# Wider value stripes: 512 columns of weights from rings of five places in the projection phase of a hybrid streaming encoder

## The chip, the cores and the metric

The kernel runs on one core of a Trainium2 chip. The metric is device time in microseconds (us) of one execution, taken as the median of several. Five engines work side by side, each with its own in-order queue: PE (TensorE, matmuls, with PEld its weight loads), DVE (VectorE), ACT (ScalarE), POOL (GpSimd) and SP (SyncE, which here issues nearly all DMAs).

## The reference

One layer of an encoder is computed for a prompt of 16 meta and 2048 prompt tokens and for 8 sample streams of 16 tokens. What matters here:

```
h = layer_norm(x, ln_in_g, ln_in_b)
(g_q, g_k, g_v, g_low, g_r, d_q, d_k, d_v, i_q, i_k, i_w, d_z, m_a, m_b) = split(h @ w_in)
o_a = gla_recurrence(g_q * DK ** -0.5, g_k, g_v, log_sigmoid(g_low @ gla_w2 + gla_gate_b) / 16)
y_a = (rms_norm(o_a) * gla_norm_g * silu(g_r)) @ w_gla
score = sum_h i_w[h] * relu(i_q[h] . layer_norm(i_k)); keep the top 256 keys of each query
y_b = (softmax_attention(d_q, d_k, d_v, kept keys) * silu(d_z)) @ w_dsa
y = layer_norm(ALPHA * h + (sigmoid(m_a + b0) * y_a + sigmoid(m_b + b1) * y_b) @ w_out)
```

The input projection `h @ w_in` has 1024 rows of contraction and 8280 columns. Its parts g_v (values), g_r (value gates) and d_z (z) have 1024 columns each.

## The kernel before

The kernel is written with a tile framework: tiles come from pools with a stated number of buffers, and a scheduler sets the order on each engine from program order, priorities (`early`, `later`) and its own estimate of when operands and places are free. All matrix products have float32 accuracy by splitting each operand into a high and a low part and adding three products (`mm3`, lines 261 to 267: high times high is L265, then the two mixed products; their sum over 8 slices of 128 rows is 24 matmuls).

Phase 1 (`phase1`, `project`) makes the input projection. The 17 blocks of 128 tokens and the 16 meta tokens lie in six pieces of three blocks or so (`PIECES`). `phase_keys` normalises and transposes every piece and makes the keys. Then three groups of two pieces each (`GROUPS`) go through all other columns. A piece's transposed tokens, high and low, stand in one of three pools xp0 to xp2 (`xtiles`, slots fixed by a list; a whole piece, all 8 slices, in one place). Two kinds of stripe exist:

- transposed stripes (`stripe_t`, `tsp`): the weights are the stationary operand, the tokens (256 or 384) stream past; used for gq, gk, q, ma, mb and the index queries;
- natural stripes (`natural`, `nat`): a block of 128 tokens is the stationary operand, 256 columns of weights stream past; used for gv, gr and z, four stripes each in every group, 6 or so blocks per stripe.

`weights` (L240) loads a stripe of w_in in four DMAs of 128x512 into `raw` (three places), casts it to `whi` on ACT (L159) and subtracts on POOL to get `wlo` (L144). Two places exist for whole stripes. Results leave PSUM through ACT (L156, L159) or DVE; for gr, POOL multiplies by gla_norm_g (L618, `silu_norm`); SP stores them.

Beside the stripes run the index scores (`index_block`, L445: matmul on PE into four PSUM places, relu on ACT, weighting on DVE) and the selection of 256 keys (`select`, a bisection by counts on DVE). They go by sets of blocks: a third or half of the group's stripes stand between one set's scores and the next (`per`).

Phase 2 (`phase2`) attends for blocks 15 to 8 (logits L1129/L1130 on PE, masks and maxima on DVE, exp on ACT, transposes L1065, values L1089). With it goes `side_work`, paced by the count of keys done: `gla_gates` (L682 matmuls with gla_w2, exp and log on ACT, scans on DVE), `attend_sample` (L1182 to L1224), the sample recurrence and 16 prompt chunks. The first 13 of its items are written with `early(EARLY)`:

```
            with self.early(EARLY):
                self.load_keys(upper, 1)
                for _ in range(NEARLY):
                    next(side)
                    items -= 1
            self.load_keys(lower, 0)
```

After block 8 the pools of the side work close, `gla_project` (tiles pd) makes y_a beside the attention of blocks 7 to 0, and `finish` does the rest (pd and fo: merges, output projection, layer norm).

Of the kernel before, what the change touches and what calls it, by code (L numbers as in the profile page):

```python
# [21 lines left out]
P = 128  # L22
# [31 lines left out]
VLATE = 60  # L54
PIECE = 720
# [64 lines left out]
class Trunk:  # L120
    def __init__(self, tc, i, o):
        self.tc, self.nc, self.i, self.o = tc, tc.nc, i, o
        self.turn = 0
        self.spare = self.flip = False
# [106 lines left out]
    def raw(self, n):  # L231
        t = self.ws.tile([P, 2 * PMAX], F32, name="raw", bufs=3)
        return t[:, : 2 * n].rearrange("p (k c) -> p k c", k=2)
# [6 lines left out]
    def weights(self, parts, pool=None, name="", eng=None):  # L240

        nc = self.nc
        width = sum(n for _, n in parts)
        w = self.i["w_in"][0].rearrange("(k p) c -> p k c", p=P)
        if pool is None:
            hi = self.ws.tile([P, KT, width], F32R, name="whi")
            lo = self.ws.tile([P, KT, width], F32R, name="wlo")
        else:
            hi = pool.tile([P, KT, width], F32R, name="whi" + name, tag="sc")
            lo = pool.tile([P, KT, width], F32R, name="wlo" + name, tag="sc")  # L250
        for q in range(4):
            s = slice(2 * q, 2 * q + 2)
            raw = self.raw(width)
            a = 0
            for c, n in parts:
                nc.sync.dma_start(raw[:, :, a : a + n], w[:, s, c : c + n])
                a += n
            self.split_sb(hi[:, s, :], lo[:, s, :], raw, eng)
        return hi, lo
# [14 lines left out]
    def prep_x(self, t, xh, xl, c, keep):  # L274
# [9 lines left out]
        for q in range(2):  # L284
# [5 lines left out]
            self.split(xh[:, s, c : c + r], xl[:, s, c : c + r], ps[:, :, :r])  # L290
# [5 lines left out]
    def nat(self, x, c, r, w):  # L296

        ps = self.pp.tile([P, 512], F32, name="pp")
        (hi, lo), (xh, xl) = w, x
        n = hi.shape[-1]  # L300
        self.mm3(ps[:r, :n], lambda k: xh[:, k, c : c + r], lambda k: xl[:, k, c : c + r],
                 lambda k: hi[:, k, :], lambda k: lo[:, k, :], KT)
        return ps[:r, :n]

    def tsp(self, x, c, n, w, a):

        ps = self.pp.tile([P, 512], F32, name="pp")
        (hi, lo), (xh, xl) = w, x
        self.mm3(ps[:, :n], lambda k: hi[:, k, a : a + P], lambda k: lo[:, k, a : a + P],
                 lambda k: xh[:, k, c : c + n], lambda k: xl[:, k, c : c + n], KT)  # L310
# [1179 lines left out]
```

## Time and profile before

| what | before |
|---|---|
| median of 3 runs | 3590.39 us (3590.21 to 3593.11) |
| profiled execution | 3593.96 us, span 3592.2 us |
| PE busy / weight loads busy | 97% / 89% of the span |
| DVE, ACT, POOL busy | 70%, 40%, 30% |
| granted PE clock, mean | 0.991 |
| DMA | 457.77 MB, mean 127 GB/s |

The page gives busy time as the union of instruction durations. On PE a matmul's duration overlaps the next one's, so the distance between two starts tells what one costs. The rows that the prediction uses stand in their own section below.

### The profile page before, as it was taken

The numbers are of one execution on the slowest core, as the hardware profiler recorded it, in microseconds if no ns is written. First come the engines' busy times: TensorE is split into PE (matmuls) and PEld (weight loads), VectorE is DVE, ScalarE is ACT, GpSimd is POOL, SyncE is SP. The second block draws the span as 40 slices with busy tenths as digits, with TensorE's granted clock in tenths as the row PEclk, the third lists the DMA queues.
The fourth block names the chain that finished last, engine by engine and source line by source line (L and its number), as shares of the span: only waits on it lengthen the run. The fifth ranks groups of instructions, "written<-read, shape, count | busy, mean of one in ns | idle before, by whom it ended". The sixth has DMA issues, their size and how long they took to land. (4 is left out here: it accounts for less than half of the span.)

```text
span 3592.2 us, 66024 instructions
## 1 busy us (share of the span) xinstructions
PE 3483.6 (97%) x24196; PEld 3212.5 (89%) x24196; DVE 2528.4 (70%) x5813; ACT 1450.9 (40%) x3092; POOL 1088.8 (30%) x1412
## 2 busy tenths in 40 slices
PE   7999999999999998999999999999999999989999
PEld 6999999999999998998887788888877888879998
DVE  7737998799999998964436677676765666544444
ACT  4435223433324323322535556566565344331110
POOL 3122242242342334434411345455410000022221
PEclk9999999999999999999999999999999999999999
DMA  8642443254442345445573433333343345564431
GB/s 265 202 131 82 139 121 108 83 157 127 119 145 73 103 134 148 140 134 159 171 199 94 122 109 97 102 105 99 100 121 88 89 120 135 151 192 136 124 115 62
DMA packets 550340, 457.77 MB, mean 127 GB/s; under 512 B 95248, under 2 KB 522528, under 8 KB 550016
## 3 DMA queue, kind: packets, MB, share of 16 engines
q1 hardware_dynamic: 550016, 453.56, 43.9%
q8 instruction: 190, 3.11, 0.4%
q14 instruction: 134, 1.10, 0.1%
HBM read 292.49 MB, written 160.92 MB: 126 GB/s over the span
## 5 line engine op out<-in xcount | busy, mean ns | idle before, releaser
L144 POOL TENSOR_TENSOR wlo<-raw,whi 128x512 fp32r<-128x512 f32 x360 | 482.3, 1360 | 817.1 <-ACT whi L159 706.7
L150 DVE TENSOR_SCALAR_CACHE_REDUCE junk<-sc,cand 128x272 bf16<-128x272 f32 (+6 forms) x512 | 701.6, 1370 | 16.9
L265 PE MATMUL pp<-whi,xh 128*128 128x256 f32 (+3 forms) x1952 | 562.1, 288 | 3.5 <-ACT whi L159 2.3
L265 PE MATMUL pp<-xh,whi 128*128 128x384 f32 (+2 forms) x1728 | 563.6, 326 | 1.9 <-ACT whi L159 1.1
L267 PE MATMUL pp<-whi,xl 128*128 128x256 f32 (+3 forms) x1952 | 560.8, 288 | 4.4 <-DVE xl L144 4.4
L267 PE MATMUL pp<-xh,wlo 128*128 128x384 f32 (+2 forms) x1728 | 563.0, 327 | 1.0 <-POOL wlo L144 1.0
L266 PE MATMUL pp<-xl,whi 128*128 128x384 f32 (+2 forms) x1728 | 563.4, 326 | 0.0
L266 PE MATMUL pp<-wlo,xh 128*128 128x256 f32 (+3 forms) x1952 | 561.9, 288 | 0.0
L265 PEld LDWEIGHTS pp<-whi,xh 128*128 128x128 f32 (+1 forms) x1952 | 371.9, 191 | 12.7 <-issue 4.3
L267 PEld LDWEIGHTS pp<-whi,xl 128*128 128x128 f32 (+1 forms) x1952 | 371.0, 190 | 11.3 <-DVE xl L144 6.9
L266 PEld LDWEIGHTS pp<-wlo,xh 128*128 128x128 f32 (+1 forms) x1952 | 371.5, 190 | 7.8 <-issue 5.2
L1131 DVE CUSTOM_DVE_ANT_0 lgl<-pl,mkl 128x348 f32<-128x348 f32 (+8 forms) x608 | 296.1, 510 | 102.8 <-PE pl L1130 65.8
L265 PE MATMUL pd<-xh,wh 128*128 128x242 f32 (+3 forms) x1152 | 327.7, 285 | 8.2 <-ACT wh L1347 4.5
L159 ACT CAST whi<-raw 128x512 fp32r<-128x512 f32 (+1 forms) x344 | 199.2, 622 | 319.7 <-DMA raw<-in_w_in 204.8
L265 PEld LDWEIGHTS pp<-xh,whi 128*128 128x128 f32 x1728 | 325.1, 188 | 3.3 <-ACT whi L159 1.7
L267 PEld LDWEIGHTS pp<-xh,wlo 128*128 128x128 f32 x1728 | 324.8, 188 | 2.5 <-POOL wlo L144 1.8
L266 PE MATMUL pd<-xl,wh 128*128 128x242 f32 (+3 forms) x1152 | 324.6, 282 | 2.1 <-DVE xl L144 2.1
L266 PEld LDWEIGHTS pp<-xl,whi 128*128 128x128 f32 x1728 | 325.1, 188 | 0.6
L267 PE MATMUL pd<-xh,wl 128*128 128x242 f32 (+3 forms) x1152 | 324.5, 282 | 0.8 <-POOL wl L144 0.8
L156 ACT ACTIVATE lgl<-lgl,mx 128x1040 f32<-128x1040 f32 (+7 forms) x256 | 249.9, 976 | 177.9 <-DVE mx L1133 171.4
L1129 PE MATMUL pl<-kd,q 128*128 128x348 f32 (+14 forms) x800 | 302.5, 381 | 14.1 <-DVE mx L1131 4.9
L1130 PE MATMUL pl<-kd,q 128*128 128x348 f32 (+14 forms) x800 | 261.7, 330 | 0.0
(252 smaller groups left out, 7592.7 us busy)
## 6 DMA issues: line engine op xcount, KB each, us to landing
raw<-in_w_in SPq DMA_DIRECT2D x360, 256.0 KB, 3.2
q<-d_q SPq DMA_DIRECT2D x272, 128.0 KB, 3.0
d_h<-x SPq DMA_DIRECT2D x17, 512.0 KB, 3.3
d_gv<-en SPq DMA_DIRECT2D x68, 128.0 KB, 1.9
d_gr<-en SPq DMA_DIRECT2D x68, 128.0 KB, 2.0
d_z<-en SPq DMA_DIRECT2D x68, 128.0 KB, 1.7
v<-d_gv SPq DMA_DIRECT2D x17, 512.0 KB, 3.7
gr<-d_gr SPq DMA_DIRECT2D x17, 512.0 KB, 3.6
```

The costliest lines, as they stand in the source:

```text
L144: (eng or self.nc.vector).tensor_tensor(out, a, b, op=op)
L150: (eng or self.nc.vector).tensor_scalar(out, a, s1, s2, op0=op0, op1=op1, **kw)
L156: self.nc.scalar.activation(out, a, f, **kw)
L159: (self.nc.vector.tensor_copy if self.spare else self.nc.scalar.copy)(out, src)
L265: mm(ps, ah(k), bh(k), start=k == 0, stop=False)
L266: mm(ps, ah(k), bl(k), start=False, stop=False)
L267: mm(ps, al(k), bh(k), start=False, stop=k == n - 1)
L1129: nc.tensor.matmul(ps[:, :m], q[:, u, :], kd, start=True, stop=False)
L1130: nc.tensor.matmul(ps[:, :m], q[:, 2 + u, :], kd, start=False, stop=True)
L1131: nc.vector.tensor_tensor_reduce(lg[z1][:, a : a + m], ps[:, :m], mk[z1][:, a : a + m], 1.0, NEG, OP.add, OP.max, mx[:, s : s + 1])
```

## The change

- gv, gr and z go in stripes of 512 columns (two per group instead of four); a block's matmul streams 512 columns and fills a PSUM bank; its eviction, its multiply on POOL and its store have 512 columns.
- Weight places hold 1024 columns' worth per partition, five high and five low (`RING`): four slices of a 256-column stripe or two slices of a 512-column stripe. A 256-column stripe takes two places, a 512-column stripe four. `raw` has four places instead of three.
- A piece's tokens lie as two halves of four slices, in one ring of five places (high and low) instead of three whole-piece pools; the fixed slots and the reversed last stripe of the second group (`flip`) go.
- The number of steps per group falls from 28 to 22, so `per` falls from 14 to 11 in the first two groups.

```diff
-        t = self.ws.tile([P, 2 * PMAX], F32, name="raw", bufs=3)
+        t = self.ws.tile([P, 2 * PMAX], F32, name="raw", bufs=RAWB)
...
-        if pool is None:
-            hi = self.ws.tile([P, KT, width], F32R, name="whi")
-            lo = self.ws.tile([P, KT, width], F32R, name="wlo")
...
+        each = 1024 // width if pool is None else KT
+        hi, lo = [], []
+        for q in range(0, KT, each):
+            for x, name in (hi, "whi"), (lo, "wlo"):
+                if pool is None:
+                    t = self.ws.tile([P, 1024], F32R, name=name, bufs=RING)
+                    x.append(t[:].rearrange("p (k c) -> p k c", c=width))
...
+            two = 2 if 2 * width <= 2 * PMAX else 1
+            for k in range(0, each, two):
+                raw = self.raw(width)[:, :two]
+                a = 0
+                for c, n in parts:
+                    nc.sync.dma_start(raw[:, :, a : a + n], w[:, q + k : q + k + two, c : c + n])
+                    a += n
+                self.split_sb(hi[-1][:, k : k + two, :], lo[-1][:, k : k + two, :], raw, eng)
...
     def xtiles(self):
-        q = self.slots.pop(0)
-        return [self.xp[q].tile([P, KT, PMAX], F32R, name="x" + n) for n in "hl"]
+
+        return list(zip(*([self.xp.tile([P, 4, PMAX], F32R, name="x" + n) for n in "hl"] for _ in range(2))))
...
-        for q in GROUPS[g][:: -1 if self.flip else 1]:
+        for q in GROUPS[g]:
...
-            self.xp = [c.enter_context(tc.tile_pool(name=f"xp{q}", bufs=1)) for q in range(3)]
+            self.xp = c.enter_context(tc.tile_pool(name="xp", bufs=5))
...
-            w = self.weights([(col, 256)])
+            w = self.weights([(col, 512)])
...
-                evac(e[:r, :256], ps)
-                nc.sync.dma_start(self.d[dst][COL[t] : COL[t] + r, col - base : col - base + 256], e[:r, :256])
+                evac(e[:r], ps)
+                nc.sync.dma_start(self.d[dst][COL[t] : COL[t] + r, col - base : col - base + 512], e[:r])
...
-            "gv": (4, lambda c: natural(C_GV + c, "gv", C_GV, True, self.copy)),
+            "gv": (2, lambda c: natural(C_GV + c, "gv", C_GV, True, self.copy)),
...
+        wide = "gv", "gr", "z"
+        steps = [lambda n=n, c=(512 if n in wide else 256) * q: step(n, c) for n in order for q in range(kinds[n][0])]
```

The scheduler makes other orders of it. Three places follow; line numbers of the change are 7 or so higher (L267, L682 and L1129 of before are L275, L689 and L1136 of the change, and the load of L976 is at L983).

First, PE where the gate matmuls (pg<-gl,w) start, before: in the last group, among the 256-column blocks of gv.

```order
L265 MATMUL pp<-whi,xh 128x256
L266 MATMUL pp<-wlo,xh 128x256
L267 MATMUL pp<-whi,xl 128x256
L682 MATMUL pg<-gl,w_20247 128x400 x2
L265 MATMUL pp<-whi,xh 16x256
```

The same place of PE in the change: the last transposed stripe of phase 1 ends, and the logits of block 15 follow.

```order
L273 MATMUL pp<-xh,whi 128x384
L274 MATMUL pp<-xl,whi 128x384
L275 MATMUL pp<-xh,wlo 128x384
L689 MATMUL pg<-gl,w_17493 128x400 x4
L1136 MATMUL pl<-kd_18595,q 128x348
L1137 MATMUL pl<-kd_18595,q 128x348
```

Before, 152 rows of the side work stand on PE ahead of the last projection matmul; in the change none does.

Second, SP around the load of gla_w2 (w), which the gate matmuls read, before: among the stores of the merge gates, with many projection loads behind it.

```order
L429 DMA d_mb<-ea 128x256 [waits DMAHW5_49,Activation_49]
L256 DMA raw<-in_w_in 128x2x256 [waits DMAHW6_49,Pool_49]
L172 DMA q<-d_q 64x4x128 [waits DMAHW7_49]
L172 DMA q<-d_q 64x4x128 [waits DMAHW0_49]
L976 DMA w_20247<-in_gla_w 16x512 [waits DMAHW1_49]
L978 DMA gb<-in_gla_gate_b 128x4x1 [waits DMAHW2_49]
L429 DMA d_mb<-ea 128x384 [waits DMAHW3_49,Activation_49]
```

And in the change: behind the last-but-one store of the query heads, right ahead of the load of the lower keys (kd), and waiting for PE.

```order
L174 DMA d_q<-eh 128x384 [waits DMAHW3_49,Activation_49]
L174 DMA d_q<-el 128x384 [waits DMAHW4_49,DVE_49]
L983 DMA w_17493<-in_gla_w 16x512 [waits DMAHW5_49,PE_49]
L985 DMA gb<-in_gla_gate_b 128x4x1 [waits DMAHW6_49]
L174 DMA d_q<-eh 128x384 [waits DMAHW7_49,Activation_49]
L174 DMA d_q<-el 128x384 [waits DMAHW0_49,DVE_49]
L989 DMA lmf<-in_c_levels 128x864 [waits DMAHW1_49]
L174 DMA kd_18595<-d_kd 128x2x1040 [waits DMAHW2_49]
```

The load has moved from the middle of the last group to the end of phase 1.

Third, PE where one gr stripe ends and the next begins (the first group of the change; pp_4967 is the last block of the old stripe, pp_5036 and pp_5065 the first two blocks of the new one, whi_4996 and whi_5006 its first two places).

```order
L275 MATMUL pp_4967<-whi_4812,xl_1921 128x512
L273 MATMUL pp_5036<-whi_4996,xh_1566 128x512
L274 MATMUL pp_5036<-wlo_4997,xh_1566 128x512
L275 MATMUL pp_5036<-whi_4996,xl_1567 128x512
L273 MATMUL pp_5036<-whi_4996,xh_1566 128x512
L274 MATMUL pp_5036<-wlo_4997,xh_1566 128x512
L275 MATMUL pp_5036<-whi_4996,xl_1567 128x512
L273 MATMUL pp_5036<-whi_5006,xh_1566 128x512
L273 MATMUL pp_5065<-whi_4996,xh_1566 128x512
L274 MATMUL pp_5065<-wlo_4997,xh_1566 128x512
L275 MATMUL pp_5065<-whi_4996,xl_1567 128x512
L274 MATMUL pp_5036<-wlo_5007,xh_1566 128x512
```

Before, the blocks of a stripe follow one another whole; in the change the first two blocks of this stripe alternate by place.

## Rows read from the trace of the kernel before

**Rows 1.** The page: span, and busy time, share and instructions of each engine.

```profile
span 3592.2 us, 66024 instructions
...
PE 3483.6 (97%) x24196; PEld 3212.5 (89%) x24196; DVE 2528.4 (70%) x5813; ACT 1450.9 (40%) x3092; POOL 1088.8 (30%) x1412
```

**Rows 2.** Stretches: from:to, length; busy by engine (x instructions); PE clock; DMA.

```profile
130.00:1370.00 1240.00, 1229.89 (x8236) 1219.46 (x8235) 1070.06 (x1632) 450.38 (x953) 399.21 (x333) 1.00 0.41 120
1450.00:1673.00 223.00, 221.36 (x1639) 220.40 (x1638) 154.26 (x387) 50.07 (x100) 84.53 (x66) 1.00 0.50 146
1673.00:1859.00 186.00, 182.91 (x1209) 163.54 (x1208) 79.71 (x154) 94.97 (x150) 65.09 (x42) 0.97 0.59 170
1877.00:2628.00 751.00, 734.66 (x5064) 608.52 (x5064) 520.10 (x1833) 444.26 (x952) 329.68 (x639) 1.00 0.37 103
2628.00:2746.00 118.00, 109.06 (x814) 88.07 (x813) 70.00 (x266) 70.76 (x155) 12.81 (x29) 0.99 0.40 108
2746.00:3164.00 418.00, 409.95 (x3319) 364.13 (x3318) 255.34 (x845) 174.21 (x386) 31.50 (x130) 1.00 0.46 122
3164.00:3592.00 428.00, 408.17 (x2629) 371.81 (x2627) 198.57 (x357) 70.65 (x147) 90.54 (x99) 0.98 0.41 127
```

**Rows 3.** One line's matmuls: count, ns min/median/max, first and last start us, forms.

```profile
L1129 PE MATMUL pl<-kd,q x800: 220/390/800, 1866.9 to 3164.0; 128*128 128x348 f32 x96, 128*128 128x344 f32 x16, 128*128 128x456 f32 x7, 128*128 128x328 f32 x7
...
L902 PE MATMUL pg<-v,kn x128: 377/379/484, 2070.8 to 2629.4; 128*128 128x256 f32 x128
```

**Rows 4.** Timeline, PE, a value stripe of 256 columns: start, duration, instruction.

```profile
500.29 0.28 PE L265 MATMUL pp<-whi,xh 128*128 128x256 f32 x1
...
501.37 0.28 PE L265 MATMUL pp<-whi,xh 128*128 128x256 f32 x1
```

**Rows 5.** Timeline, PE, last stage, 512 columns.

```profile
3559.66 0.39 PE L265 MATMUL fo<-woh,mgh 128*128 128x512 f32 x1
...
3561.93 0.39 PE L266 MATMUL fo<-wol,mgh 128*128 128x512 f32 x1
```

**Rows 6.** PE by line and shape, whole run: xcount, busy us, mean ns, idle.

```profile
L265 PE MATMUL pp<-whi,xh 128*128 128x256 f32 x1632 | 464.9, 285 | 0.3 <-DVE el L144 0.3
```

**Rows 7.** PE groups by line and shape, 1673 to 1859 us.

```profile
L265 PE MATMUL pp<-whi,xh 128*128 128x256 f32 x121 | 36.0, 298 | 0.0
L265 PE MATMUL pp<-xh,whi 128*128 128x384 f32 x96 | 33.0, 344 | 0.0
...
L265 PE MATMUL pp<-xh,whi 128*128 128x256 f32 x96 | 27.1, 283 | 0.0
L682 PE MATMUL pg<-gl,w 16*128 16x512 f32 x24 | 13.4, 640 | 0.9 <-DVE gx L150 0.9
L265 PE MATMUL pp<-whi,xh 128*16 128x256 f32 x24 | 6.7, 277 | 0.0
```

**Rows 8.** Timeline, PE, a transposed stripe, 384 columns.

```profile
401.81 0.33 PE L267 MATMUL pp<-xh,wlo 128*128 128x384 f32 x1
...
402.68 0.33 PE L266 MATMUL pp<-xl,whi 128*128 128x384 f32 x1
```

**Rows 9.** POOL by line and shape, 0 to 1700 us.

```profile
L144 POOL TENSOR_TENSOR wlo<-raw,whi 128x512 fp32r<-128x512 f32 x332 | 442.9, 1354 | 755.6 <-ACT whi L159 665.2 <-DVE whi L159 20.2 <-PE pi L446 18.9
L144 POOL TENSOR_TENSOR en<-en,gng 128x256 f32<-128x256 f32 x68 | 54.5, 802 | 113.0 <-ACT en L156 108.3 <-DMA cd<-in_cache_idx_k 3.4 <-DMA raw<-in_w_in 1.3
```

**Rows 10.** DMA issues: queue, count, KB each, median us to landing.

```profile
raw<-in_w_in SPq DMA_DIRECT2D x360, 256.0 KB, 3.2
```

**Rows 11.** Waits of PE, 0 to 1900 us: total, times, longest.

```profile
PE pi L445 <- ACT rl L156: 18.8, 14, 4.2
```

**Rows 12.** Timeline, PE, end of the projections: [idle before <-releaser].

```profile
1858.72 0.34 PE L267 MATMUL pp<-xh,wlo 128*128 128x384 f32 x1
...
1866.89 0.66 PE L1129 MATMUL pl<-kd,q 128*128 128x348 f32 x1 [2.62 <-DMA kd<-d_kd]
```

**Rows 13.** ACT by line and shape, 1673 to 1859 us.

```profile
L156 ACT ACT_TABLE_LOAD x21 | 26.9, 1283 | 0.4
```

More of the change, by code (lines that the diff above doesn't have):

```diff
@@ L54 @@
 VLATE = 60
+RING = 5
+RAWB = 4
 PIECE = 720
@@ L123, in __init__ @@
         self.turn = 0
-        self.spare = self.flip = False
+        self.spare = False
     @contextmanager
@@ L231, in raw @@
     def raw(self, n):
-        t = self.ws.tile([P, 2 * PMAX], F32, name="raw", bufs=3)
-        return t[:, : 2 * n].rearrange("p (k c) -> p k c", k=2)
+        t = self.ws.tile([P, 2 * PMAX], F32, name="raw", bufs=RAWB)
+        two = 2 if n <= PMAX else 1
+        return t[:, : two * n].rearrange("p (k c) -> p k c", k=two)
     def split_sb(self, hi, lo, src, eng=None):
@@ L244, in weights @@
         w = self.i["w_in"][0].rearrange("(k p) c -> p k c", p=P)
-        if pool is None:
-            hi = self.ws.tile([P, KT, width], F32R, name="whi")
-            lo = self.ws.tile([P, KT, width], F32R, name="wlo")
[L248 to L259, printed above, removed]
+        each = 1024 // width if pool is None else KT
[5 more added lines that the diff above has]
+                    x.append(t[:].rearrange("p (k c) -> p k c", c=width))
+                else:
+                    x.append(pool.tile([P, KT, width], F32R, name=name + str(width), tag="sc"))
+            two = 2 if 2 * width <= 2 * PMAX else 1
[6 more added lines that the diff above has]
+                self.split_sb(hi[-1][:, k : k + two, :], lo[-1][:, k : k + two, :], raw, eng)
+        return (lambda k: hi[k // each][:, k % each, :]), (lambda k: lo[k // each][:, k % each, :]), width
     def mm3(self, ps, ah, al, bh, bl, n):
@@ L289, in prep_x @@
             s = slice(4 * q, 4 * q + 4)
-            self.split(xh[:, s, c : c + r], xl[:, s, c : c + r], ps[:, :, :r])
+            self.split(xh[q][:, :, c : c + r], xl[q][:, :, c : c + r], ps[:, :, :r])
             if keep is not None:
@@ L579, in phase1 @@
             self.inb = self.bcast_load(kp, i["idx_kn_b"][0], 64, "inb")
-            self.x, self.slots = {}, [0, 1, 2, 0, 1, 2, 0, 1, 2, 1]
+            self.x = {}
             self.phase_keys()
@@ L596, in project @@
                     nc.sync.dma_start(raw, self.d["xt"][q][:, k : k + 2, :])
-                    self.split_sb(xh[:, k : k + 2, :n], xl[:, k : k + 2, :n], raw)
+                    r = slice(k % 4, k % 4 + 2)
+                    self.split_sb(xh[k // 4][:, r, :n], xl[k // 4][:, r, :n], raw)
         tiles = [(t, q) for q in GROUPS[g] for t in PIECES[q]]
@@ L634, in step @@
             self.spare = g == len(GROUPS) - 1 and n in SPARE
-            self.flip = g == len(GROUPS) - 2 and (n, c) == (order[-1], 256 * (kinds[n][0] - 1))
             kinds[n][1](c)
-            self.spare = self.flip = False
-        steps = [lambda n=n, c=256 * q: step(n, c) for n in order for q in range(kinds[n][0])]
+            self.spare = False
+        wide = "gv", "gr", "z"
+        steps = [lambda n=n, c=(512 if n in wide else 256) * q: step(n, c) for n in order for q in range(kinds[n][0])]
         blocks = [t for t, _ in tiles if t not in ("m", "s", 0)]
```

19 lines of the change are left out of this document (9 added, 10 removed).

## The prediction

> **What bounds the kernel now.** I read the page first, then busy time by stretch, then the start times on PE, then the waits. The page shows PE busy 97% of the span and its weight loads 89% [rows 1], but the share is not the same everywhere. Cut into stretches [rows 2], the projection phase from 130 to 1370 us and from 1450 to 1673 us has matmuls busy 99% and weight loads 98% to 99% at a granted clock of 1.00 (the 2.4 GHz level): there PE is the bound, and a matmul saved is time saved. Phase 2's attention runs from the first logits at 1866.9 us to the last at 3164.0, and the side work's last prompt chunk ends near 2629 [rows 3]. From 1877 to 2628 us, attention with side work, matmuls still read 98% (734.7 of 751) but weight loads only 81% (608.5 of 751); from 2746 to 3164 us weight loads are at 87%.
>
> What a matmul costs is the distance between two starts. In a value stripe of 256 columns nine distances take 501.37 - 500.29 = 1.08 us, 0.120 us each [rows 4]. In the last stage, with 512 columns and the same 128x128 stationary operand, ten take 2.27 us, 0.227 us each [rows 5]. So two of 256 cost 0.240 us and one of 512 costs 0.227: 0.013 us is a fixed part that a matmul pays whatever its width.
>
> **Term 1, the wider stripes: -32 us.** Three products of 1632 matmuls of 256 columns stand in the trace [rows 6], 4896 in all. The change makes 2448 of 512 columns: 2448 x 0.013 = 31.8 us less. The work lies where PE is the bound. Bounds: none of it if the fixed part comes back as a wait, 32 if all stays.
>
> The page "TensorE: Matmul & The Clock Gate" of the Trainium skill, section Back-to-back issue gap, gives a fixed part of 2.5 ns per matmul when the array is warm; by that the term would be 2448 x 2.5 ns = 6 us instead of 32. The starts in the trace measure 13 ns here, and they decide.
>
> **Term 2, the end of phase 1 loses its guests: -49 us.** This is not in the diff but in the order of the instructions. Before, the load of gla_w2 stands among the last group's projections, and gate and sample-attention matmuls run between projection matmuls; in the change the load waits for PE at the end of phase 1 and no row of the side work stands ahead of the last projection matmul. What the guests take now: in the 186 us from 1673 to 1859 us [rows 2] PE has three products of about 121 natural matmuls, 96 transposed ones of 384 columns, 96 of 256 and 24 for the meta rows [rows 7]. At 0.120 us for 256 columns and 0.87/5 = 0.174 us for 384 [rows 8] that is 363 x 0.120 + 288 x 0.174 + 288 x 0.120 + 72 x 0.120 = 137 us. The other 49 us are guests and the waits around them, and leave phase 1.
>
> **Term 3, the guests' new place: +35 us.** The same work comes back beside the attention of blocks 15 to 8, pushes the remaining side work later, and so pushes the first pass of gla_project, whose pools open when the side work's close, into the stretch after it. Lower bound 0: weight loads leave 19% of 751 us free there, 142 us. Upper bound on PE 49, on ACT more (rival B). I take 35, nearer the upper end, for two reasons: gla_project's displaced pass lands between 2746 and 3164 us, where weight loads are at 87%, and matmuls that wait for each other's results through ACT and DVE do not pack.
>
> The page "Perfetto Trace Analysis" of the Trainium skill, section Identifying the Most-Contended Engine, says that matmul busy time is a bad measure of headroom, since matmuls are pipelined, and that weight-load busy time is a good one. By matmul time (98%) the term would be the full 49, by weight loads (81%) it could be 0. The trace shows the two columns apart; no row here shows which of them tells the room.
>
> **Term 4, weights from a ring of five: +5 us.** Before, a whole stripe stands ready ahead. Now a 512-column stripe takes four of five places, so only a quarter of the next one can stand ready. A block takes 24 x 0.227 = 5.4 us; in the old stripe's last block a place falls free every 1.36 us, and each needs two POOL subtractions of 1.354 us [rows 9] behind a cast. Counting from that block's start: the first refill is ready near 5 us, the next at 7.7; on gr POOL also has a multiply of 2 x 0.80 = 1.6 us per block [rows 9], which pushes the last slice to about 12.2; its load of 3.2 us [rows 10] must wait for a raw place and is about as late. PE would want that slice at 5.4 + 7 x 0.68 = 10.2 us if blocks went one by one, 2 us too early. But the order alternates the first two blocks there, which puts that slice near 15 us. Six wide stripes in three groups make 18 starts; at 0 to 2.7 us each the bounds are 0 and 49. I take 5, near the lower end, because of the alternation. POOL's total is no issue: 8 x 1.35 + 6 x 1.6 = 20 us in a gr stripe of 32.7 us.
>
> **Term 5, scores and selection: +3 us.** PE waits 18.8 us in 14 times for relu on ACT [rows 11], whose three places (`score`, L453) DVE frees. DVE's work is unchanged and it is busy 86% of 130 to 1370 us [rows 2]. PE arrives about 21 us earlier at the last group (two thirds of term 1), so the wait can grow by up to 20; the order puts the second set's scores elsewhere, so it can also shrink by 10. I take +3.
>
> **Term 6, the seam: +5 us.** Between the last projection matmul and the first logits 8.2 us pass now, ended by the load of kd [rows 12], partly filled with guests. In the change the small load of gla_w2 goes ahead of kd on SP, the first gate matmuls stand ahead of the logits on PE and wait for it, and nothing fills the gap. Bounds 0 and +10.
>
> **At nothing.** Evictions, multiplies and stores of 512 columns: half as many, on engines that wait for PE; their cover is PE's own 32.7 us per stripe. The token halves: one half of the next group's tokens can be loaded ahead instead of a whole piece; the rest is split while PE works at the old last piece (two transposed blocks of 24 x 0.174 = 8.3 us) against two subtractions per half. If that fails, 2 or 3 us at two group changes. A fourth raw place gains up to 1 us at the start.
>
> **Sum.** -32 - 49 + 35 + 5 + 3 + 5 = -33 us. Against the profiled execution, 3594.0 us, that is 3561. The runs' median is 3590.4, 3.6 below it, so **3557 us**. About 0.2%, 7 us, is what a measurement can tell from no change.
>
> **Rivals.**
>
> A, the guests find room (13%): term 3 is 0, because attention is paced by DVE and ACT and PE's free 142 us take them. For it: weight loads at 81%. Against it: the displaced pass of gla_project. Time: 3557 - 35 = 3522 us.
>
> B, the guests cost ACT more than they cost PE, and the kernel gets slower (15%). Place: the first attention blocks. In 1673 to 1859 us ACT is busy 95.0 us; at the 50.1/223 of the stretch before, the projection alone would need 42 [rows 2], so the guests hold ACT for at least 53 us and at most 95, of which 26.9 are 21 table loads of 1.28 us [rows 13]. In 1877 to 2628 us ACT is already busy 59%, with exps that PE's transposes wait for. If every guest instruction of ACT delays an exp, term 3 is about 74 instead of 35: 3557 + 39 = 3596 us. It turns to a loss once term 3 is above 68. Against it: ACT has 307 us free there.
>
> C, the ring starves PE (7%): 18 starts at 2.7 us, 49 instead of 5: 3601 us. It decides when PE wants the last place before about 12 us; the waits of PE would name POOL or ACT at the stripes' starts.
>
> D, the fixed part per matmul is not saved in this phase (5%): a matmul of 512 columns takes 0.240 us here, term 1 is 0, and the time 3557 + 32 = 3589 us. Against it: [rows 4] and [rows 5] are the same instruction at the same clock. By the Trainium skill's 2.5 ns ("TensorE: Matmul & The Clock Gate", Back-to-back issue gap) it would be 3583.
>
> That the change doesn't do what it says is ruled out by the order, which shows 512 columns in the stripes.
>
> **How the numbers follow.** The forecast has 60%. Its own range from the bounds of terms 3 to 6 is 3525 to 3587. The range of 3522 to 3596 takes in A and B and leaves out most of C and the far tails, under 2 in 10. Faster than 3583: nearly all of the forecast (58), A (13), some of B and C (5), 76%. Slower than 3598: half of B (8) and most of C (5), 13%. Between, within 0.2%: D and the rest, 11%.
>
> **What would show it.** Term 1: natural groups of 816 matmuls per product with starts 0.227 us apart. Term 2: the last projection matmul ends near 1859 - 32 - 49 + 8 = 1786 us, with no gate matmul ahead of it. Term 3: the logits of block 15 start some 75 us earlier than now, but the attention's end (now 3164 us) only some 40 earlier; if it is 75 earlier, A is right; if it is not earlier at all, B. Term 4: PE's waits for wlo and whi stay under 10 us in all. Term 5: the wait for relu stays near 19 us. If the last projection matmul ends later than 1810 us, terms 1, 4 or 5 are wrong.

## The result and the profile after

The changed kernel takes **3627.52 us** (median of 4 runs, 3624.85 to 3630.71) against 3591.75 of the kernel before in the same comparison: ratio 1.0098, interval 1.0086 to 1.0111. It is 1.0% slower, where the prediction said 3557 us and allowed 3522 to 3596. The profiled execution has a span of 3623.2 us, 31.0 more than before [rows 1].

The page of the changed kernel, where PE does some 2500 matmuls fewer than in [rows 1] and is busy as long:

```profile
span 3623.2 us, 60680 instructions
...
PE 3487.0 (96%) x21700; PEld 3088.4 (85%) x21700; DVE 2521.0 (70%) x5801; ACT 1442.3 (40%) x3000; POOL 1078.5 (30%) x1378
```

First and last starts of line groups on PE in the changed kernel: the last projection matmuls, the logits (L1129 before), and the chunk update of the gated work (L902 before), to be read against [rows 3] and [rows 12].

```profile
L275 PE MATMUL pp<-xh,wlo x1728: 276/334/522, 183.9 to 1793.2; 128*128 128x384 f32 x159, 128*128 128x256 f32 x30, 128*128 128x272 f32 x3
...
L1136 PE MATMUL pl<-kd,q x800: 219/402/796, 1807.3 to 3192.4; 128*128 128x348 f32 x96, 128*128 128x344 f32 x16, 128*128 128x456 f32 x7, 128*128 128x328 f32 x7
...
L909 PE MATMUL pg<-v,kn x128: 377/379/484, 2207.6 to 2756.8; 128*128 128x256 f32 x128
```

Phase 1 ends at 1793.2 us, 65.5 before the old 1858.7: as forecast, nearly (1786). The logits start 59.6 us earlier (1866.9 to 1807.3) and end 28.4 us *later* (3164.0 to 3192.4). So from first to last logits phase 2 takes 1385.1 us where it took 1297.1. All the loss lies there; the stretch behind it is 431 us, before 428.

Where the first guests (the matmuls of the decay gates) stand on PE, in the kernel before and in the changed one, and in the same order the first product of the gated outputs' projection (`gla_project`):

```profile
L682 PE MATMUL pg<-gl,w x40: 374/587/692, 1673.3 to 1747.3; 16*128 16x512 f32 x24, 16*128 16x400 f32 x8, 16*128 16x256 f32 x8
L689 PE MATMUL pg<-gl,w x40: 374/692/1217, 1795.6 to 1893.4; 16*128 16x512 f32 x24, 16*128 16x400 f32 x8, 16*128 16x256 f32 x8
...
L265 PE MATMUL pd<-xh,wh x1152: 218/278/580, 2673.0 to 3552.0; 128*128 128x242 f32 x86, 128*128 128x256 f32 x86, 128*128 128x240 f32 x10, 128*128 128x128 f32 x10
L273 PE MATMUL pd<-xh,wh x1152: 218/278/582, 2797.9 to 3583.0; 128*128 128x242 f32 x86, 128*128 128x256 f32 x86, 128*128 128x240 f32 x10, 128*128 128x128 f32 x10
```

The stretches of the changed kernel, columns as in [rows 2]:

```profile
130.00:1370.00 1240.00, 1221.66 (x6540) 1139.72 (x6540) 1058.15 (x1608) 447.82 (x888) 402.82 (x313) 0.99 0.41 121
1465.00:1793.00 328.00, 328.00 (x1988) 304.60 (x1987) 168.31 (x416) 67.50 (x126) 112.58 (x89) 1.00 0.46 137
1793.00:1950.00 157.00, 133.36 (x695) 91.77 (x694) 98.69 (x274) 118.83 (x179) 25.24 (x25) 0.83 0.48 138
...
2050.00:2757.00 707.00, 691.98 (x4715) 568.30 (x4713) 490.68 (x1766) 410.28 (x915) 327.26 (x640) 1.00 0.39 106
...
2798.00:3193.00 395.00, 385.56 (x3135) 346.65 (x3134) 225.93 (x737) 151.22 (x343) 29.02 (x117) 0.99 0.48 127
3193.00:3623.00 430.00, 409.36 (x2648) 373.05 (x2646) 199.40 (x357) 70.73 (x147) 90.75 (x99) 0.97 0.42 127
```

The line from 1793 to 1950 us is new: for 157 us behind the projections PE's weight loads are at 58%, ACT is busy 76%, POOL 16%, and the granted clock is 0.83, so that part of the stretch was at the lower level, 1.2 GHz. In the line of the side work (2050 to 2757) PE looks just as before. The side work itself simply stands 127 us later (2629.4 to 2756.8).

The seam between the two phases of the changed kernel, PE's timeline; before, one wait of 2.62 us stood here [rows 12]:

```profile
1793.20 0.34 PE L275 MATMUL pp<-xh,wlo 128*128 128x384 f32 x1
1795.63 1.58 PE L689 MATMUL pg<-gl,w 16*128 16x400 f32 x4 [2.09 <-DMA w<-in_gla_w]
1801.08 3.03 PE L689 MATMUL pg<-gl,w 16*128 16x400 f32 x4 [3.88 <-DVE gx L152]
1807.33 0.63 PE L1136 MATMUL pl<-kd,q 128*128 128x348 f32 x1 [3.22 <-DMA q<-d_q]
```

The wide stripes themselves did as forecast. PE's group of them, and the first and last of eight in a row: seven distances in 1.60 us, 0.229 us each (0.227 in [rows 5]):

```profile
L273 PE MATMUL pp<-whi,xh 128*128 128x512 f32 x816 | 313.4, 393 | 0.0
```

```profile
922.28 0.40 PE L273 MATMUL pp<-whi,xh 128*128 128x512 f32 x1
...
923.88 0.39 PE L274 MATMUL pp<-wlo,xh 128*128 128x512 f32 x1
```

Some of PE's waits to 1793 us in the changed kernel (us in total, times, longest): for relu hardly more than in [rows 11], for weights 3.2 and 1.4 us.

```profile
PE pi L451 <- ACT rl L158: 20.2, 15, 3.6
...
PE pp L273 <- ACT whi L161: 3.2, 2, 2.5
...
PE pp L275 <- POOL wlo L146: 1.4, 1, 1.4
```

### The profile page after: what moved, and what is told of

Its sections match the earlier page's. It is cut to its first block, busy times and chain, and to the rows that moved or that the text cites. A ratio compares the mean times of both kernels' runs of the same rounds, so it can differ in the third digit from the quotient of the medians.

```text
span 3623.2 us, 60680 instructions
## 1 busy us (share of the span) xinstructions
PE 3487.0 (96%) x21700; PEld 3088.4 (85%) x21700; DVE 2521.0 (70%) x5801; ACT 1442.3 (40%) x3000; POOL 1078.5 (30%) x1378
## 5 line engine op out<-in xcount | busy, mean ns | idle before, releaser
L152 DVE TENSOR_SCALAR_CACHE_REDUCE junk<-sc,cand 128x272 bf16<-128x272 f32 (+6 forms) x512 | 701.6, 1370 | 16.8
L275 PE MATMUL pp<-xh,wlo 128*128 128x384 f32 (+2 forms) x1728 | 562.6, 326 | 1.5 <-POOL wlo L146 1.4
L275 PE MATMUL pp<-whi,xl 128*128 128x512 f32 (+3 forms) x1120 | 413.4, 372 | 10.1 <-DVE xl L146 9.9
L273 PE MATMUL pp<-whi,xh 128*128 128x512 f32 (+3 forms) x1120 | 408.1, 372 | 4.3 <-ACT whi L161 2.5
L274 PE MATMUL pp<-wlo,xh 128*128 128x512 f32 (+3 forms) x1120 | 411.1, 370 | 0.0
L273 PE MATMUL pd<-xh,wh 128*128 128x242 f32 (+3 forms) x1152 | 328.4, 286 | 12.8 <-ACT wh L1354 8.5
L1136 PE MATMUL pl<-kd,q 128*128 128x348 f32 (+14 forms) x800 | 309.7, 390 | 24.8 <-DVE mx L1138 11.5
L275 PEld LDWEIGHTS pp<-xh,wlo 128*128 128x128 f32 x1728 | 324.7, 188 | 2.8 <-POOL wlo L146 2.2
L275 PE MATMUL pd<-xh,wl 128*128 128x242 f32 (+3 forms) x1152 | 324.1, 282 | 0.5 <-POOL wl L146 0.5
L155 DVE SCALAR_TENSOR_TENSOR sc<-rl,iw,sc 128x388 f32<-128x388 f32 (+16 forms) x308 | 216.1, 738 | 81.2 <-ACT rl L158 80.3
L1072 PE MATMUL px<-ident,lgl 128*128 128x128 f32 x1600 | 253.6, 281 | 13.9 <-ACT lgl L158 6.1
L1137 PE MATMUL pl<-kd,q 128*128 128x348 f32 (+14 forms) x800 | 265.2, 335 | 0.0
L1096 PE MATMUL oo<-pt,v 128*64 128x256 f32 x1088 | 257.4, 384 | 3.1 <-ACT pt L1080 2.3
```

Source lines behind the costliest of these rows:

```text
L152: (eng or self.nc.vector).tensor_scalar(out, a, s1, s2, op0=op0, op1=op1, **kw)
L155: self.nc.vector.scalar_tensor_tensor(out, a, s, b, op0=op0, op1=op1)
L273: mm(ps, ah(k), bh(k), start=k == 0, stop=False)
L274: mm(ps, ah(k), bl(k), start=False, stop=False)
L275: mm(ps, al(k), bh(k), start=False, stop=k == n - 1)
L1072: nc.tensor.transpose(ps[:, 2 * s + u, :], pe[u][a // KLOW][:, a % KLOW : a % KLOW + P], self.ident[:])
```

## The experiments

The theory after this comparison, called *cover* below: the guests (decay gates and sample attention) cost little beside the projections and far more in front of the attention, and the change took their place away. Their tiles lie on memory that the old pools of pieces left free in the last group; the new ring of half pieces holds that memory to the end of phase 1. The rivals were the stripes and rings themselves, the way phase 2 starts, and the bunching of 13 side steps at its head.

### Cover taken from the kernel before, and given back to the changed one

**e1_before_no_room**, on the kernel before:

```diff
-            self.x, self.slots = {}, [0, 1, 2, 0, 1, 2, 0, 1, 2, 1]
+            self.x, self.slots = {}, [0, 1, 2, 0, 1, 2, 0, 1, 2, 0]
...
-            self.flip = g == len(GROUPS) - 2 and (n, c) == (order[-1], 256 * (kinds[n][0] - 1))
```

> The kernel before, with one thing changed: in the last group the first piece of tokens takes pool 0 in place of pool 2 (and the order of the last stripe ahead of it is not turned round), so that the memory on which the guests' tiles lie is taken to the end of phase 1, as in the changed kernel; its listing has every gate product behind the last projection product. Theory cover (the guests cost what they took from nothing before): phase 1 ends some 35 to 50 us earlier, the last logits come some 100 us of phase 2 later, and the time is the 3592 of before plus the 36 us that the change cost plus the 32 us that its wider stripes saved: 3660 us, 3640 to 3675. By my prediction's terms 2 and 3 (-49 and +35) it would be 3578. Rival stripes (the rings and the wide stripes cost the time, the guests little): 3580 to 3600.

Measured: 3633.36 us, ratio 1.0114 (1.0096 to 1.0132). Starts on PE in this kernel, the same three groups and the gates:

```profile
L267 PE MATMUL pp<-xh,wlo x1728: 276/334/594, 178.6 to 1805.3; 128*128 128x384 f32 x159, 128*128 128x256 f32 x30, 128*128 128x272 f32 x3
...
L1128 PE MATMUL pl<-kd,q x800: 219/397/792, 1807.3 to 3198.0; 128*128 128x348 f32 x96, 128*128 128x344 f32 x16, 128*128 128x456 f32 x7, 128*128 128x328 f32 x7
...
L901 PE MATMUL pg<-v,kn x128: 377/379/483, 2217.1 to 2762.8; 128*128 128x256 f32 x128
...
L681 PE MATMUL pg<-gl,w x40: 374/587/1056, 1810.2 to 1906.4; 16*128 16x512 f32 x24, 16*128 16x400 f32 x8, 16*128 16x256 f32 x8
```

The gates start behind the last projection matmul, as in the changed kernel. Phase 1 ends 53.4 us earlier, phase 2 takes 1390.7 us instead of 1297.1. With the old stripes and the old weight tiles, taking the room away costs as much as the whole change does. The figure is below the 3660 that I expected, because I had put the wide stripes at 32 us; e3 shows what they are worth.

**e2_after_room**, on the changed kernel: the pools of the guests lie lowest, the upper keys and the probabilities' pool on the ring.

```diff
-            upper = [left(f"kdu{q}") for q in range(2)]
-            self.stu = left("stu")
             gc = self.gla_pools(early)
...
             self.sb = left("sb")
+            upper = [left(f"kdu{q}") for q in range(2)]
+            self.stu = left("stu")
```

> The changed kernel with one thing changed: the left pools of phase 2 are opened in another order, those of the guests and of the side work first, then the upper keys and the probabilities' pool, so that the guests lie on what the index work frees (scores, index queries, key tiles) and none on the ring of tokens' pieces. Its listing has all gate products and nearly all of the sample attention ahead of the last projection product again. Theory cover: the time is that of before less the wider stripes' 32 us, 3560 us, 3545 to 3575, with the last projection product near 1825 and the last logits near 3135. Rival stripes: as the changed kernel, 3615 to 3630, since the stripes and rings are untouched. A cost of its own could be the upper keys, which can be loaded only when the ring is free: some 5 to 10 us at the seam.

Measured: 3624.59 us, ratio 1.0091 (1.0074 to 1.0109): as the changed kernel. Starts on PE: the last projection matmul, and the first product of the gated outputs' projection.

```profile
L275 PE MATMUL pp<-xh,wlo x1728: 275/334/522, 184.5 to 1847.5; 128*128 128x384 f32 x159, 128*128 128x256 f32 x30, 128*128 128x272 f32 x3
...
L273 PE MATMUL pd<-xh,wh x1152: 218/278/582, 2788.7 to 3581.9; 128*128 128x242 f32 x86, 128*128 128x256 f32 x86, 128*128 128x240 f32 x10, 128*128 128x128 f32 x10
```

The guests are back and phase 1 is 54 us longer, but two things that I had not priced, or too low, go with it. The logits start only at 1875.8 us, 28 behind the last projection: all the upper keys now lie on the ring, so that their loads are issued only from 1847.9 us on, and most of the sample attention that is left runs ahead of the logits. And the projection's weights lie on the upper keys' memory, which the attention holds until block 8 is done; its first product stands at 2788.7 us instead of 2673.0 (2655.7 in f5, where they do not lie there). The time misses the theory's number, and since the layout costs something of its own, it does not test the theory either.

**f5_wide_with_room**, the changed kernel with a layout that avoids both:

```diff
-            self.xp = c.enter_context(tc.tile_pool(name="xp", bufs=5))
+            self.xp, self.place = [c.enter_context(tc.tile_pool(name=f"xp{q}", bufs=1)) for q in range(5)], 0
...
-            upper = [left(f"kdu{q}") for q in range(2)]
+            upper = [left("kdu0"), None]
...
+            upper[1] = inner.enter_context(tc.tile_pool(name="kdu1", bufs=1, side="right"))
...
-        first = [next(ws) for _ in range(6)]
+        first = [next(ws) for _ in range(5)]
```

> The changed kernel with its memory laid out anew: the ring of tokens' pieces as five places with pools of their own, taken in turn, so that the lowest is free in the last group; of phase 2's pools only the upper keys of the second pair of heads, which the first block needs last, and the gated state lie over the ring, and the weights of the projection of the gated outputs lie on the guests' memory as before (in e2_after_room they had to wait for the upper keys). Its listing has all gate products and nearly all sample attention ahead of the last projection product, and the first product of that projection 150 rows behind the last side product (before: 200; changed kernel: 150; e2: 900). Theory cover: before less the 11 us by which the wide stripes end phase 1 earlier: 3582, 3572 to 3592. Rival stripes (something else in the changed kernel slows it): 3610 to 3630.

Measured: 3611.64 us, ratio 1.0062 (1.0043 to 1.0080). By the ratios 13 of the 36 us come back, by the medians 16, and not 45: phase 1 ends at 1849.0 us as expected, but the logits run from 1867.0 to 3178.0, a seam of 18 us and 1311 us for 1297.

**g1_whole_pieces_ring4** and **g2_whole_pieces_ring5**: wide stripes in the memory of the kernel before, whole pieces in three pools again.

```diff
-RING = 5
-RAWB = 4
+RING = 4
+RAWB = 3
...
-            self.xp = c.enter_context(tc.tile_pool(name="xp", bufs=5))
+            self.xp = [c.enter_context(tc.tile_pool(name=f"xp{q}", bufs=1)) for q in range(3)]
```

> The stripes of 512 columns in exactly the memory of the kernel before: three pools of whole pieces with their order and turn, the weight ring cut to four places and the raw blocks to three. One wide stripe fills the ring, so the next can follow only as its last tile frees the places. Its listing has the guests where the kernel before has them. Theory cover: the guests cost their covered price, the wide stripes bring the 11.5 us that they brought between e3 and the changed kernel, less what the short ring costs; from 18 wide stripes at 0 to 2 us of wait each that is 0 to 36: 3580 to 3615, centre 3590. Theory stripes (wide stripes hurt by themselves): above 3610.

Measured: 3601.40 us, ratio 1.0023 (1.0012 to 1.0033). Starts on PE, and its longest waits for weights to 1850 us:

```profile
L275 PE MATMUL pp<-xh,wlo x1728: 276/334/522, 180.6 to 1850.1; 128*128 128x384 f32 x159, 128*128 128x256 f32 x30, 128*128 128x272 f32 x3
...
L1139 PE MATMUL pl<-kd,q x800: 222/394/795, 1856.1 to 3171.3; 128*128 128x348 f32 x96, 128*128 128x344 f32 x16, 128*128 128x456 f32 x7, 128*128 128x328 f32 x7
```

```profile
PE pp L273 <- ACT whi L161: 8.2, 7, 2.4
```

Four places and three raw blocks cost 8.2 us of waits for the high parts where five and four cost 3.2. The guests have their old cover, and 26 of the 36 us are back. The logits start 10.8 us before those of the kernel before, and end 7.3 us after.

g2 had five places for the high parts, four for the low, and two raw blocks of 512 columns:

```diff
-RAWB = 4
+RAWB = 2
...
-        t = self.ws.tile([P, 2 * PMAX], F32, name="raw", bufs=RAWB)
+        t = self.ws.tile([P, 512], F32, name="raw", bufs=RAWB)
...
-                    t = self.ws.tile([P, 1024], F32R, name=name, bufs=RING)
+                    t = self.ws.tile([P, 1024], F32R, name=name, bufs=RING - (name == "wlo"))
```

> As g1_whole_pieces_ring4, with five places for the high parts and four for the low ones, paid for by two raw blocks of 512 columns in place of three of 768, so that pieces and weights come in one contraction row of blocks at a time. Theory cover: 3578 to 3600, centre 3585; what it lies under g1 is what the fifth place is worth, and waits for raw blocks (transfers that stand behind the split of the block before) could take that back.

Measured: 3655.85 us, ratio 1.0177 (1.0162 to 1.0191), outside what I expected. Phase 1 ends at 1908.5 us, 58 behind that of g1. Its longest wait on PE to 1908 us, and ACT's group of casts from 150 to 1850 us with what ended its idle time:

```profile
PE pp L273 <- ACT whi L161: 42.9, 15, 10.8
```

```profile
L161 ACT CAST whi<-raw 128x512 fp32r<-128x512 f32 x319 | 197.9, 621 | 589.8 <-DMA raw<-in_w_in 575.0 <-PE pp L275 9.7 <-PE pp L274 4.6
```

PE waits for casts, and these for transfers into raw blocks: 575.0 us of ACT's idle time before them, where the same group of g1 has 196.7. Against g1 the blocks were the scarce thing, not the places.

### What the guests cost in either place

**f2_no_guests**, on e1_before_no_room; it leaves out the guests' products and their work on ACT and DVE, and stores zeros:

```diff
-                    nc.tensor.matmul(ps[:, :n], self.w2[:, h * P : (h + 1) * P], gl[:, :n], start=True, stop=True)
...
+            x = self.sb.tile([P, 2, 512], F32, name="gx", tag="s4", bufs=SKB)
+            nc.gpsimd.memset(x[:], 0.0)
```

> e1_before_no_room without the guests' arithmetic: the decay gates and the sample attention write zeros to where their results go (as many transfers out, no product, no ACT or DVE work). It gives the guests' price in either place: before minus this is what they cost beside phase 1, e1_before_no_room minus this what they cost in phase 2. Theory cover: 3535 to 3550, that is 45 to 55 us under phase 1 (my term 2 had 49) and 85 to 95 us in phase 2 (my term 3 had 35). Rival start (the loss is in how phase 2 starts without cover: keys, queries and a cold clock, whatever the guests do): 3570 to 3605.

Measured: 3535.17 us, ratio 0.9852 (0.9834 to 0.9870). So beside the projections the guests cost 1.5% of 3590, 53 us (47 to 60 by the interval); in front of the attention (e1 less f2: 1.0114 - 0.9852) 2.6%, 94 us. Both prices take f2 as the kernel without guests, so the 41 us between them are e1's own loss. And the first place is not wholly beside the projections: in the kernel before, half of the sample attention's value products, 32 of 64, start behind the last projection matmul, to 1928 us. Rival *start* is out: it wanted at least 3570 us. Starts on PE in f2, whose phase 2 begins without cover and takes 1304.9 us, 8 more than that of the kernel before:

```profile
L267 PE MATMUL pp<-xh,wlo x1728: 276/334/424, 179.0 to 1801.8; 128*128 128x384 f32 x159, 128*128 128x256 f32 x30, 128*128 128x272 f32 x3
...
L1107 PE MATMUL pl<-kd,q x800: 222/392/801, 1803.5 to 3108.4; 128*128 128x348 f32 x96, 128*128 128x344 f32 x16, 128*128 128x456 f32 x7, 128*128 128x328 f32 x7
...
L880 PE MATMUL pg<-v,kn x128: 376/379/485, 1999.1 to 2550.9; 128*128 128x256 f32 x128
```

The same 243 us in f2 (first) and in e1:

```profile
1807.00:2050.00 243.00, 225.68 (x1433) 177.03 (x1435) 160.74 (x528) 129.18 (x249) 82.91 (x155) 0.97 0.51 153
```

```profile
1807.00:2050.00 243.00, 219.83 (x1351) 161.46 (x1352) 159.02 (x496) 175.22 (x304) 29.09 (x37) 0.91 0.42 116
```

With the guests ACT works 46 us more and POOL 54 us less: the prompt chunks, whose factors POOL makes, have hardly begun. Their last update stands at 2762.8 us in e1 and at 2550.9 in f2, 212 us apart. The clock is lower too, 0.91 for 0.97.

**e4_after_not_early**, on the changed kernel:

```diff
-NEARLY = 13
+NEARLY = 0
```

> The changed kernel with no side step put ahead of the attention's start: all 31 are given out between the attention's steps. Rival bunching (the guests cost much because 13 steps stand together at the start of phase 2, where the PE waits for the ACT and DVE work of each; spread out they would lie beside logits): 3580 to 3605. Theory cover in its strict form (the guests' work on ACT, DVE and PE is simply added to a stretch that has no room): 3615 to 3640, the stretch 1793 to 1950 loses less and later ones more.

Measured: 3633.75 us, ratio 1.0115 (1.0099 to 1.0130). But the trace shows that the edit did not spread the guests. The gates' matmuls on PE:

```profile
L689 PE MATMUL pg<-gl,w x40: 374/587/1218, 1792.2 to 1895.6; 16*128 16x512 f32 x24, 16*128 16x400 f32 x8, 16*128 16x256 f32 x8
```

That is where they stand in the changed kernel (1795.6 to 1893.4). The last value product of the sample attention starts at 2070.0 us (2057.9 there), still ahead of the prompt chunks, and the last chunk update at 2761.1. So this run does not test the rival *bunching*, and no other run does: what the guests would cost spread out among the attention's steps stays open.

### What the wide stripes are worth

**e3_after_256**, on the changed kernel, rings kept:

```diff
-            w = self.weights([(col, 512)])
+            w = self.weights([(col, 256)])
...
-            "gv": (2, lambda c: natural(C_GV + c, "gv", C_GV, True, self.copy)),
+            "gv": (4, lambda c: natural(C_GV + c, "gv", C_GV, True, self.copy)),
```

> The changed kernel with both rings, but values, value gates and z again in stripes of 256 columns. Theory cover: the guests stay late, and the 32 us of the wide products (1632 x 2 of 256 columns at 0.120 us against half as many of 512 at 0.227) are lost: 3660 us, 3645 to 3670. Rival stripes (the wide stripes starve on the ring of five places, or wait elsewhere): faster than the changed kernel, 3590 to 3620.

Measured: 3632.18 us, ratio 1.0113 (1.0098 to 1.0128), which fits neither expectation. Its last projection matmul:

```profile
L275 PE MATMUL pp<-xh,wlo x1728: 276/334/440, 182.3 to 1804.7; 128*128 128x384 f32 x159, 128*128 128x256 f32 x30, 128*128 128x272 f32 x3
```

It equals e1 to 1.2 us in the median and to 0.6 at the end of phase 1 (1805.3): the two rings cost nothing there. (Its seam is 13.6 us, e1's 2.0, and its phase 2 is 5 us shorter.) The wide stripes bring 11.5 us at the end of phase 1 (1804.7 to 1793.2) and 4.7 us in the medians (the two intervals overlap), where I had 32.

**f3_wide_no_selection** and **f4_narrow_no_selection**, on the changed kernel and on e3:

```diff
-                self.select(items)
+                for t, *_ in items:
+                    self.open_mask(t)
```

> The changed kernel without the bisection of the index scores (the 32 counting passes and the ties of each set, all on DVE); every block gets the mask that leaves all keys open. Read against f4_narrow_no_selection, the same with stripes of 256 columns. Theory DVE (in phase 1 the relus wait on ACT for score sums that stand behind counting passes on DVE, and the wide stripes leave less PE work between the sets, so that 18 of their 32 us come back as such waits): without the passes the last projection product comes 28 to 33 us earlier here than in f4, where it is 11.5 us earlier with them. Rival weights (the wide stripes lose it on their ring or in their pitch): still 10 to 15 us.

> The changed kernel with stripes of 256 columns and without the bisection of the index scores, masks left open. Both theories: the waits for relus in phase 1 shrink from some 17 us to under 5; its last projection product lies near 1790. What tells them apart is the difference to f3_wide_no_selection.

Measured: 3593.39 us, ratio 1.0001 (0.9988 to 1.0015), and 3611.00, ratio 1.0063 (1.0046 to 1.0080). Both leave the selection out, so they tell only what it costs. The last projection matmul of f3 and of f4:

```profile
L275 PE MATMUL pp<-xh,wlo x1728: 276/334/445, 184.5 to 1757.2; 128*128 128x384 f32 x159, 128*128 128x256 f32 x30, 128*128 128x272 f32 x3
```

```profile
L275 PE MATMUL pp<-xh,wlo x1728: 276/334/445, 182.2 to 1781.5; 128*128 128x384 f32 x159, 128*128 128x256 f32 x30, 128*128 128x272 f32 x3
```

They are 24.3 us apart, not 11.5; a little under the 28 that I expected, twice what the rival *weights* gave. So the selection costs phase 1 36.0 us with wide stripes (1793.2 - 1757.2) and 23.2 with narrow ones (1804.7 - 1781.5). From 130 to 1370 us DVE falls from 85% in the changed kernel to 24% in f3:

```profile
130.00:1370.00 1240.00, 1236.65 (x6648) 1154.57 (x6647) 293.05 (x498) 453.21 (x902) 405.89 (x320) 1.00 0.42 126
```

How the selection holds PE shows in the timeline of the changed kernel, DVE first, then ACT and PE:

```profile
1152.33 2.20 DVE L547 TENSOR_TENSOR_SCAN cs<-eq,ties 128x456 f16<-128x456 bf16 x1
...
1154.46 1.62 DVE L155 SCALAR_TENSOR_TENSOR eq<-sc,cand,eq 128x456 bf16<-128x456 f32 x1
1156.01 0.66 DVE L155 SCALAR_TENSOR_TENSOR sc<-rl,iw,sc 128x432 f32<-128x432 f32 x1
...
1156.76 0.53 ACT L158 ACTIVATE rl<-pi 128x432 f32<-128x432 f32 x1 [4.92 <-DVE sc L155]
...
1157.34 0.73 PE L451 MATMUL pi<-kih,iq 128*128 128x432 f32 x1 [3.51 <-ACT rl L158]
...
1158.65 0.63 PE L273 MATMUL pp<-whi,xh 128*128 128x512 f32 x1
1159.08 0.63 PE L274 MATMUL pp<-wlo,xh 128*128 128x512 f32 x1
...
1163.33 0.39 PE L273 MATMUL pp<-whi,xh 128*128 128x512 f32 x1
1163.56 0.40 PE L274 MATMUL pp<-wlo,xh 128*128 128x512 f32 x1
```

The score sum (sc) stands on DVE behind the ties of the set before, the relu waits for its place, and PE for the relu. Behind this wait PE's matmuls run slower: the wide ones take 0.63 us and start 0.43 us apart, and some 5 us later again 0.39 and 0.23. The stretch around it has a granted clock of 0.88, so that part of it was at 1.2 GHz and not at 2.4:

```profile
1150.00:1164.00 14.00, 10.49 (x42) 8.65 (x41) 13.81 (x17) 5.95 (x13) 8.62 (x5) 0.88 0.45 125
```

### Is the rest a matter of order?

With the room back, g1 ends phase 1 by 8.6 us earlier than the kernel before (1850.1 for 1858.7), and yet takes 8 us longer; its phase 2 is 18 us longer. One edit in two kernels asked whether that is the order of the query loads:

```diff
-        q = self.qload(self.aq, c, h0, bufs=AQB)
+        with self.early(400):
+            q = self.qload(self.aq, c, h0, bufs=AQB)
```

> g1_whole_pieces_ring4 with the loads of the attention's queries given out earlier (priority by 400 steps). In g1 the first logits come 10.8 us before those of the kernel before, the last 7.3 us after: phase 2 is 18 us longer, 4.9 of it a wait for a query load that stands on SP behind the sample attention's stores. Theory queue (the wide stripes' gain is lost at that seam): 3585 to 3595, about 3588. Theory order (the list order of phase 2 is another one whenever phase 1 ends differently, and the kernel before has a good one): 3595 to 3615, the gain of the earlier queries lost elsewhere.

> The kernel before with the same edit and nothing else: the same instructions on every engine, in another order from the attention's start on. Theory queue: 3585 to 3592, a little faster, since its own seam waits 2.6 us for keys and not for queries. Theory order: slower, 3597 to 3612; the size of that is what an arrangement of phase 2 is worth that nobody chose.

Measured: h1 3601.87 us, ratio 1.0036 (1.0023 to 1.0050); h2 3588.92, ratio 1.0004 (0.9995 to 1.0013). Neither kernel moved. The query loads are not the cause, and this re-ordering is worth nothing to the kernel before, so the theory *order* has no support from it. What makes phase 2 longer in f5 and g1 (1311 and 1315 us for 1297) stays open.

## Why the prediction was wrong

The end came out on rival B's side and beyond it. By the prediction's own terms, in the profiled executions:

| term | predicted | measured | from |
|---|---|---|---|
| 1 and 5, stripes with scores and selection | -32 + 3 | -11.5 | e3 to after, last projection matmul |
| 2, phase 1 loses its guests | -49 | -53.4 | before to e1 |
| 3, guests in phase 2 | +35 | +88 | first to last logits, 1385.1 - 1297.1 |
| 4, rings | +5 | -0.6 | e1 to e3, 1805.3 and 1804.7 |
| 6, seam | +5 | +5.9 | 14.1 - 8.2 |

The measured terms add up to +28; with the 3 us of the last stretch that is the 31 between the spans. The range that the prediction calls its own, 3525 to 3587, is not what its bounds give: those of terms 3 to 6, added up, reach from 3499 to 3637, and 3627 lies inside.

**Term 3 is the step that failed**, by 53 us: the price of the guests in phase 2, taken at 35 and measured at 88. Its mechanism was named rightly: the guests push the side work later and with it the first pass of gla_project (2673.0 us before, 2797.9 after). Its size was wrong, and so was its bound. "Upper bound on PE 49" took the guests' own PE time for the most they could cost; f2 and e1 measured 94 us for work that costs 53 beside the projections. The row in which I saw room, weight loads at 81% [rows 2], did not tell room. Guests that run first hold back everything behind them: gates and sample attention stand ahead of the prompt chunks, which end 212 us later in e1 than in f2, and ACT is at 72% of that first stretch. Their 21 table loads [rows 13] go with them: the changed kernel has as many from 1793 to 1950 us, f2 has one from 1803 to 2004.

```profile
L158 ACT ACT_TABLE_LOAD x21 | 26.9, 1283 | 3.3 <-issue 2.9
```

Not all of the 88 need be the guests. From f2 to e1 phase 2 grows by 86 us (1304.9 to 1390.7), which is theirs; f2 without them and without cover has 8 more than the kernel before, and f5 and g1, which have the guests' room, 14 and 18 more for a reason that stays open.

**Rival B** had the right direction and place and too low a price: 74 for term 3, from ACT alone, where 88 was measured. I gave it 15% because ACT had 307 us free; free time summed over 751 us says nothing of the first 150. How the 41 us between the guests' two prices divide between ACT, the lower clock, the bunching and the chunks' late start, no run tells apart. **Rival A** is out by its own sign: the attention's end had to come 75 us earlier and comes 28 later.

Neither of the two measures that the prediction weighed there gave the price: 0 by weight-load time and 49 by matmul time; the runs are above both. The Trainium skill ("Perfetto Trace Analysis", Identifying the Most-Contended Engine) names the first, with the share of peak FLOPs, for judging TensorE's headroom; here it did not give the price of added work. The Trainium skill ("Perfetto Trace Analysis", Optimization Strategy) says that where the most-contended engine changes over time, interleaving those regimes may gain. Here PE is the busiest engine on either side of the seam, and what differs is ACT: 22% from 1450 to 1673 us [rows 2], 53% at the head of f2's phase 2, where no guests are. Starting the guests in the first place was worth 41 us, which is what e1 lost.

**Terms 1 and 5** together were off by 17.5 us. The wide matmuls take the time that [rows 5] said. Without the selection they save 24.3 us, 9.9 ns for each of 2448, where I had 13 from two distances rounded to a nanosecond; and with the selection's load on DVE 12.8 of the 24.3 us are gone again. I had the bound of term 5 (+20) and its mechanism right, and took +3. I expected it in one row, the relu waits; that row went from 17.9 (e3) to 20.2 us only. All of PE's waits in phase 1 together are 52.3 us in the changed kernel and 46.6 in e3, 28.8 in f3 and 31.6 in f4: that makes 8.5 of the 12.8. The rest I can't name wait by wait; from 130 to 1370 us the granted clock is 0.99 in the changed kernel and 1.00 in the three others. The fixed part of 2.5 ns that the Trainium skill states, there for the gap of a matmul on its own ("TensorE: Matmul & The Clock Gate", Back-to-back issue gap), would make 6 us by estimate; f3 and f4 show four times that.

**Terms 2, 4 and 6** held (4 was taken at +5 and came out at nothing). Rivals C and D are out: waits for weights are 4.6 us, and the stripes do save their fixed part, as far as DVE lets them.

## What to carry to other kernels

Before you change the shape of a pool, find what later tiles lie on its memory and what work starts early because of that; the price of losing such cover is not the work's own time on the bound engine but what it costs at the head of the next phase, here nearly twice that. Measure it directly: leave the work out once, with the cover gone, and take the kernel's time with it in either place. And where a second engine is as busy as DVE here (85%), a saving on the bound engine is worth only what that engine lets through: here 24 us without its load, 11.5 with it.

## What the runs showed that I had not expected

- A waiting PE can pay twice: after the wait of 3.5 us in the timeline above its matmuls ran at the lower clock for some 4 us. In 88 us at the start of the changed kernel's phase 2, after waits of 2.1, 3.9 and 3.2 us at the seam and with weight loads at 49%, the granted clock is 0.72; whether the waits alone kept it there no run shows:

```profile
1798.00:1886.00 88.00, 70.72 (x263) 43.01 (x264) 52.38 (x129) 72.36 (x95) 20.95 (x15) 0.72 0.50 160
```

- A weight ring of four places with wide stripes of four (g1) costs PE only 8.2 us of waits, while one raw block fewer and smaller ones (g2) cost 42.9. Between these two, how early transfers can start mattered more than how many finished places there are.
- No version with the wide stripes that does all the work beat the kernel before. The nearest, g1, has the wide stripes in the old memory, with the guests in their old place, and is still 0.23% (0.12 to 0.33%) slower. So the room is most of the loss, 26 of 36 us, and not all of it.
